# Modulation products, mLSTM weights and weight remainders placed elsewhere in a hybrid decoder layer

## The chip, the cores and the metric

One core of one Trainium2 chip runs the whole layer in one launch. The metric is device time in microseconds, the median of repeated runs. The engines are named as in the profile: PE (TensorE, matmuls), PEld (its weight loads), DVE (VectorE), ACT (ScalarE), POOL (GpSimd), SP (SyncE, which issues most of the transfers). Each engine, and each queue of transfers, takes its instructions in the order of the program; between engines semaphores carry the dependences.

## The reference

One decoder layer on x of 1024 positions by 1024 channels, everything in float32:

```
mod = silu(c) @ w_ada + b_ada                       # 6 rows of 1024: sh1 sc1 g1 sh2 sc2 g2
h   = rms_norm(x) * (1 + sc1) + sh1
proj = h @ w_in                                     # q,k of the mLSTM | v | o | gates | attention q | k,v
q_ml, k_ml = silu(causal conv of width 4 over positions)
h_ml = mLSTM(q_ml, k_ml, v_ml, gates)               # 4 heads of 128, max-stabilised
o_at = sliding window attention (8 heads of 64, window 128, rotary, sinks)
x   = x + g1 * rms_norm(concat(norms) @ w_out)
h   = rms_norm(x) * (1 + sc2) + sh2
x   = x + g2 * rms_norm((gelu(conv3(h @ w_up gate)) * conv3(h @ w_up value)) @ w_down)
```

The mLSTM's output for position t of a chunk is num / max(|den|, exp(-m_t)). In it the weight of an earlier position s is exp(b_t - b_s + i_s - m_t), and that of the state carried from earlier chunks is exp(b_t + m - m_t), where b is the running sum of the forget gate's logarithm and m_t the running maximum.

## The kernel before

Matrix products are made of float32 operands split into a part that TensorE takes in one pass (hi, a cast on ScalarE) and a remainder (lo = value - hi, a subtraction). `mm3` (L87) adds three products for each pair: hi by hi, hi by lo, lo by hi. So each weight tile of the input projection (a "unit", 128 x 1024, loaded whole by SP in `w_unit`, L139) needs a cast on ScalarE and a remainder, which units 0 to 9 form on VectorE and units 10 to 21 on GpSimd (L193). Raw, hi and lo tiles have three buffers each, so a unit takes the slot of the unit three before it.

The modulation vector is 48 columns of 128 values. `ada_sum` (L163) forms one of them on VectorE: it multiplies a 128 x 1024 tile of the transposed `w_ada` by silu(c), broadcast to all partitions in `cb`, and accumulates along the row.

The stages, in order:

1. Front (L197 to L411), in an order written out by hand on all engines (`manual_schedule`). Blocks of 128 positions of x are squared on ScalarE, scaled on VectorE (L261), transposed on TensorE (L265) and copied out of PSUM by both (L268). Two modulation sums, columns 8 and 0, end in `shift_gain` (L270); then the first 128 channels are modulated (L282), split and multiplied (L88 to L90). After that the channels go in eight chunks (`h_chunk`), with two sums, two splits and 48 matmuls each, for the attention's k and v and half of the mLSTM's v.
2. First token group (units 4 and 5: other half of v, gates). Keys are rotated (`rope`, VectorE and GpSimd), transposed and split in `kv_evac` (L449), all blocks ahead of the group's code.
3. Attention in two groups of four heads (units 6, 7 and 8, 9). After each block's front (`att_front`) one, in the second group two, modulation sums run in the background (`ada_bg`, L365: a load on SP into one of two buffers, and a sum). In the second group the gates are formed: `gates_rows` (L609) on 32 rows (head by block) and `gates_columns` (L653), which turns them into columns `gcol`. The row u = -max(...) goes to DRAM and returns broadcast to all partitions.
4. Four mLSTM heads (L771 to L783): two units with 512-column matmuls each, a convolution of four taps on ScalarE and VectorE (L690 to L695), and `ml_head` (L698). For each group of four blocks it forms the weights dm and qw (GpSimd addition, mask, ScalarE exponential, GpSimd multiplication), sq and kw on VectorE, and then block by block the numerator with its denominator column (`tot`), the state's increment (`st`), the state C on VectorE (L741, L743), and copies of `tot`: the numerator on ScalarE (L745), the denominator on VectorE (L746), the numerator's square on ScalarE (L748). Eight modulation sums stand between (L775, L781).
5. Output gates and output projection; then the feed-forward part, with seven products in place of eight.

Outside the stretches written by hand, a planner lays out each engine's order in advance, by simulated times and the order of the code; on the chip every engine keeps that order. `order(later, earlier)` adds a condition to it.

## Time and profile before

| | |
|---|---|
| median of 3 runs | 1149.92 us (1146.79 to 1153.52) |
| profiled execution | 1150.41 us, span 1148.7 us |
| mean granted TensorE clock | 0.991 |
| busy: PE, DVE, ACT, POOL | 97%, 75%, 49%, 18% of the span |

Windows and starts are microseconds from the start of the span. A group's row shows the line, engine and operation, the tiles (output <- inputs) with their shapes, the count, then busy time and mean nanoseconds of one, and last the idle time of the engine ahead of it with what ended it. A wait's row reads "who waited <- for whom: total, times, longest". A line of the timeline has start, duration, instruction, and in brackets the idle time before it.

### The profile page before, as it was taken

To read this page: it belongs to the slowest core of one execution; us is meant where nothing else is said; L and a number is where in the kernel's file an instruction comes from. 1 tells how busy PE (TensorE), PEld (TensorE's weight loads), DVE (VectorE), ACT (ScalarE), POOL (GpSimd) and SP (SyncE) were. 2 spreads that over 40 slices of the span, in tenths; PEclk is the share of its full clock that TensorE was granted. 3 is DMA by queue.
4 is the path that set the end of the run, shared out by engine and by line. 5 is a ranking of instruction groups with operands and counts; after the bars stand their busy time and mean duration, and the time that the engine had idled before them with its cause. 6 is when DMAs were issued, how large, how long until landed. Compare 5 with 4: busy or idle time off the path is not lost.

```text
span 1148.7 us, 16112 instructions
## 1 busy us (share of the span) xinstructions
PE 1114.7 (97%) x5919; PEld 941.1 (82%) x5919; DVE 857.9 (75%) x1501; ACT 564.1 (49%) x1112; POOL 203.8 (18%) x259
## 2 busy tenths in 40 slices
PE   6999999999999999999999999999999999999997
PEld 5999998777789888877788888888888888787885
DVE  6945889678764456799998797879787875787666
ACT  5642634524544446475554444545454554445552
POOL 3021447576665200000000000000000000000021
PEclk8999999999999999999999999999999999999999
DMA  9622445062111412333342233133313458553545
GB/s 359 237 83 75 130 123 186 25 202 70 42 37 35 150 74 92 110 95 107 120 121 81 92 127 111 57 118 119 120 56 110 141 194 289 169 173 119 173 119 200
DMA packets 54462, 144.72 MB, mean 126 GB/s; under 512 B 5304, under 2 KB 5616, under 8 KB 54384
## 3 DMA queue, kind: packets, MB, share of 16 engines
q1 hardware_dynamic: 52496, 138.19, 36.1%
q10 hardware_dynamic: 1888, 5.51, 1.2%
q8 instruction: 46, 0.75, 0.3%
q14 instruction: 32, 0.26, 0.1%
HBM read 115.09 MB, written 28.60 MB: 125 GB/s over the span
## 4 chain that ended last, share of the span: by engine, by line
PE 78%; DVE 12%; DMA 4%; ACT 2%; issue 2%; POOL 1%; SPq 1%; DVEq 0%; POOLq 0%; ACTq 0%
PE X L1005 7%; PE X L1004 7%; PE X L1003 7%; PE Y L1005 4%; PE Y L1003 4%; PE Y L1004 4%; DVE ada L164 3%; PE tg L88 3%; PE y L88 3%; PE y L90 3%; PE y L89 3%; PE tg L89 3%; PE tg L90 3%; DMA rb<-in_w_down_dram 2%; PE Z L1005 1%
## 5 line engine op out<-in xcount | busy, mean ns | idle before, releaser
L93 POOL TENSOR_SCALAR rsb<-ssb 128x1 f32<-128x1 f32 x4 | 2.3, 583 | 611.4 <-ACT junk L1228 611.2
L164 DVE SCALAR_TENSOR_TENSOR ada<-ada,cb 128x1024 f32<-128x1024 f32 x48 | 64.5, 1351 | 7.4 <-DMA ada<-in_w_ada_dram 7.2
L1003 PE MATMUL X<-S,wl 128*128 128x512 f32 x156 | 62.4, 400 | 0.0
L1005 PE MATMUL X<-S,wl 128*128 128x512 f32 x156 | 61.9, 396 | 0.0
L1004 PE MATMUL X<-S,wl 128*128 128x512 f32 x156 | 61.7, 395 | 0.0
L1013 DVE SCALAR_TENSOR_TENSOR yg<-ug,cv,yg 128x1023 f32<-128x1023 f32 (+1 forms) x44 | 56.4, 1281 | 5.7 <-ACT yg L1010 5.7
L85 ACT CAST wl<-T 128x512 fp32r<-128x512 f32 x41 | 25.5, 621 | 66.5 <-PE X L1004 62.6
L1013 DVE SCALAR_TENSOR_TENSOR yv<-uv,cv,yv 128x1023 f32<-128x1023 f32 (+1 forms) x44 | 56.3, 1278 | 1.9 <-ACT yv L1010 1.9
L85 ACT CAST w<-T 128x512 fp32r<-128x512 f32 x47 | 29.1, 623 | 40.7 <-PE Z L1005 34.7
L85 DVE TENSOR_TENSOR w<-T,w 128x512 fp32r<-128x512 f32 x47 | 32.1, 687 | 16.6 <-ACT w L85 16.6
L1057 DVE TENSOR_TENSOR uv<-q,X 128x512 f32<-128x512 f32 x22 | 15.1, 686 | 38.4 <-PE X L1005 38.4
L85 DVE TENSOR_TENSOR A<-ra,A 128x512 fp32r<-128x512 f32 x46 | 31.7, 689 | 15.9 <-ACT A L85 15.4
L85 ACT CAST A<-ra 128x512 fp32r<-128x512 f32 x46 | 28.6, 621 | 28.8 <-PE dxu L1177 14.2
L85 ACT CAST B<-rb 128x512 fp32r<-128x512 f32 x44 | 27.2, 619 | 31.0 <-DMA rb<-in_w_down_dram 13.9
L85 DVE TENSOR_TENSOR B<-rb,B 128x512 fp32r<-128x512 f32 x44 | 30.3, 689 | 10.0 <-ACT B L85 9.5
L1005 PE MATMUL Y<-S,wl 128*128 128x512 f32 x92 | 36.4, 396 | 0.0
L85 ACT CAST wl<-fu 128x512 fp32r<-128x512 f32 x21 | 13.0, 621 | 47.6 <-PE Y L1004 44.6
L1003 PE MATMUL Y<-S,wl 128*128 128x512 f32 x92 | 36.4, 395 | 0.0
L1004 PE MATMUL Y<-S,wl 128*128 128x512 f32 x92 | 36.2, 394 | 0.0
L1004 PEld LDWEIGHTS X<-S,wl 128*128 128x128 f32 x156 | 29.3, 188 | 7.6 <-issue 0.5
L1003 PEld LDWEIGHTS X<-S,wl 128*128 128x128 f32 x156 | 29.3, 188 | 7.5 <-issue 0.5
L1005 PEld LDWEIGHTS X<-S,wl 128*128 128x128 f32 x156 | 29.3, 188 | 7.1
(614 smaller groups left out, 4012.9 us busy)
## 6 DMA issues: line engine op xcount, KB each, us to landing
ada<-in_w_ada_dram SPq DMA_DIRECT2D x48, 512.0 KB, 4.4
ra<-a_dram SPq DMA_DIRECT2D x30, 512.0 KB, 3.7
fu<-in_w_up_dram SPq DMA_DIRECT2D x26, 512.0 KB, 3.6
a_dram<-yg SPq DMA_DIRECT2D x22, 512.0 KB, 3.7
rb<-in_w_down_dram SPq DMA_DIRECT2D x44, 256.0 KB, 3.6
fu_False<-in_w_up_dram SPq DMA_DIRECT2D x18, 512.0 KB, 3.6
a_dram<-s SPq DMA_DIRECT2D x11, 512.0 KB, 5.4
x<-in_x_dram SPq DMA_DIRECT2D x8, 512.0 KB, 7.3
```

The source lines that it names most:

```text
L85: return A.copy(hi, src), eng.tensor_tensor(lo, src, f(hi), op=ALU.subtract)
L88: T.matmul(ps, lh, rh, start=first, stop=False)
L89: T.matmul(ps, lh, rl, start=False, stop=False)
L90: return T.matmul(ps, ll, rh, start=False, stop=last)
L93: G.tensor_scalar(dst, ssq, 1.0 / n, EPS, op0=ALU.mult, op1=ALU.add)
L164: return V.scalar_tensor_tensor(w, w, 0.5, cb, op0=ALU.mult, op1=ALU.mult, accum_out=mod[:, j : j + 1])
L1003: T.matmul(ps, w[:, 0, ks], a[:, 0, k, :], start=st, stop=False, skip_group_check=True)
L1004: T.matmul(ps, w[:, 0, ks], a[:, 1, k, :], start=False, stop=False, skip_group_check=True)
L1005: ends = T.matmul(ps, w[:, 1, ks], a[:, 0, k, :], start=False, stop=en, skip_group_check=True)
L1013: V.scalar_tensor_tensor(t[:, sh:], src[:, : S - sh], w(tap), t[:, sh:], op0=ALU.mult, op1=ALU.add)
L1057: V.tensor_tensor(uv[:, 512:], p5, px_, op=ALU.add)
```

## The change

It has five parts.

- The front: columns 8 and 0 of the modulation are matrix products on TensorE (`ada_product`: for each of them eight matmuls of 128 x 128 by one column), with c loaded a second time as columns and the tiles of `w_ada` for these two laid out otherwise on the host. Three of the copies of the transposed x move from VectorE to ScalarE, the last of them behind the split of the first chunk.
- Key rotation (`k_turn`) and key split (`k_split`) stand inside the first token group's evacuation, block by block, with VectorE's order written out there; eight modulation sums stand there too, in place of those between the heads, and the splits of units 6 and 7 at its blocks 3 and 6.
- The remainders of units 10 to 21 are formed on VectorE.
- The mLSTM's second weight, exp(u + m), is formed once on 32 rows, and both rows are written to DRAM and broadcast, into two buffers; the mask is applied in place to the broadcast u, one instruction per head; the first weight is the exponential with the column a as bias, four instructions of 128 columns per group.
- The denominator is copied with the numerator by ScalarE, and VectorE takes its absolute value per block.

Two conditions of order are new: the gates' logarithm behind a mark of the first attention group's sixth block, and unit 8's remainder behind that of its third.

```diff
@@ -143,7 +146,7 @@
             s = slice(i * n, (i + 1) * n)
-            split(hi[:, s], lo[:, s], raw[:, s], eng)
+            rests[name] = split(hi[:, s], lo[:, s], raw[:, s], eng)[1]
         return hi, lo
@@ -190,7 +194,7 @@
             else:
-                units.append(w_unit(w_in[u if u < 4 else u - 2], 1024, f"w{u}", (G if u >= 10 else V,)))
+                units.append(w_unit(w_in[u if u < 4 else u - 2], 1024, f"w{u}"))
@@ -233,6 +237,7 @@
     nc.scalar.dma_start(ch8, c.rearrange("o (k m) -> (o k) m", k=KD))
+    nc.scalar.dma_start(cc8, ccol)
     x_load(0)
@@ -289,6 +294,9 @@
     V.scalar_tensor_tensor(ch8, th8, 1.0, ch8, op0=ALU.add, op1=ALU.mult)
+    A.activation(tc8, cc8, AF.Tanh, scale=0.5)
+    V.scalar_tensor_tensor(cc8, tc8, 1.0, cc8, op0=ALU.add, op1=ALU.mult)
+    V.tensor_scalar(cc8, cc8, 0.5, None, op0=ALU.mult)
     cbs = []
@@ -302,19 +310,29 @@
     x_evac(0, 1, D_)
+    mps = []
+    def ada_product(j):
+        if not mps:
+            mps.append(pA("mod0"))
+        for k in range(KD):
+            T.matmul(mps[0][:, j : j + 1], adas[j][:, k * P : (k + 1) * P], cc8[:, k : k + 1], start=k == 0, stop=k == KD - 1)
     for b in range(2, NB):
...
         x_evac(b - 2, 0, C_)
-        x_evac(b - 1, 1, D_)
+        x_evac(b - 1, 1, D_ if b < 6 else C_)
         if b == 5:
...
             V.scalar_tensor_tensor(gb, cv[:, C_BADA + 8 : C_BADA + 16], 1.0, cv[:, C_PREMIX : C_PREMIX + 8], op0=ALU.add, op1=ALU.mult)
-            ada_sum(8, adas[8])
+            ada_product(8)
         if b == 6:
-            ada_sum(0, adas[0])
-            shift_gain(0)
+            ada_product(0)
+    V.tensor_tensor(mod[:, 0:1], mps[0][:, 0:1], cv[:, C_BADA : C_BADA + 1], op=ALU.add)
+    V.scalar_tensor_tensor(g_mix[:, 0:1], mps[0][:, 8:9], cv[:, C_PREMIX : C_PREMIX + 1], gb[:, 0:1], op0=ALU.mult, op1=ALU.add)
     h0, h1 = h_part(0, 0), h_part(0, 1)
@@ -328,8 +346,8 @@
     h1[2]()
-    x_evac(7, 1, D_)
     h1[3]()
+    x_evac(7, 1, C_)
@@ -446,13 +464,18 @@
-    def kv_evac(b, ps):
-        kr = ap_.tile([P, 256], F32, tag="qr", bufs=2, name=f"kr{b}")
+    krs = {}
+    def k_turn(b):
+        ps = pkv[b // 2][:, 256 * (b % 2) : 256 * (b % 2 + 1)]
+        kr = krs[b] = ap_.tile([P, 256], F32, tag="qr", bufs=2, name=f"kr{b}")
         rope(kr[:, :P].rearrange("p (h t f) -> p h t f", h=2, t=2),
...
         A.copy(vat[:, b, :, :64], ps[:, P : 2 * P].rearrange("p (v d) -> p v d", v=2))
+    def k_split(b):
         pk = pB(f"pk{b}")
-        T.transpose(pk[:, :P], kr[:, :P], ident)
+        T.transpose(pk[:, :P], krs[b][:, :P], ident)
         ts = slice(b * P, (b + 1) * P)
@@ -543,21 +566,31 @@
+    second = tc.manual_schedule(engines={mybir.EngineType.DVE})
+    second.__enter__()
     ensure(6)
...
         v_evac(b, 1, pv[b // 2][:, 256 * (b % 2) : 256 * (b % 2 + 1)])
-    for b in range(NB):
-        kv_evac(b, pkv[b // 2][:, 256 * (b % 2) : 256 * (b % 2 + 1)])
     def v_gates(b, ps):
...
         A.copy(gates.rearrange("p (g b) -> p g b", g=8)[:, :, b], ps[:, 256:264])
+        if b + 2 < NB:
+            k_turn(b + 2)
+        k_split(b)
+        if b == 6:
+            ensure(8)
+        ada_bg(ap_)
+        if b == 3:
+            ensure(7)
...
         G.memset(mix_v(b)[:, :, HD : HD + 1], vscale)
+    k_turn(0)
+    k_turn(1)
     token_group(4, VG, v_gates)
     V.tensor_tensor(gates.rearrange("p (g b) -> p g b", g=8), gates.rearrange("p (g b) -> p g b", g=8), bc(rw[:, 0:8], 2, [P, 8, NB]), op=ALU.add)
-    ensure(7)
+    ensure(8)
+    second.__exit__(None, None, None)
@@ -579,9 +612,8 @@
-    ensure(8)
     att_group(6, 0)
-    gcol = cp.tile([P, 5, 32], F32, name="gcol")
+    gcol = cp.tile([P, 4, 32], F32, name="gcol")
@@ -592,7 +624,7 @@
-    V.scalar_tensor_tensor(tA, gf_, -1.0, gf_, op0=ALU.mult, op1=ALU.min)
+    order(V.scalar_tensor_tensor(tA, gf_, -1.0, gf_, op0=ALU.mult, op1=ALU.min), marks[5])
     A.activation(tA, tA, AF.Exp)
@@ -641,7 +674,10 @@
         V.tensor_scalar(urow, crow, mprev, -1.0, op0=ALU.max, op1=ALU.mult)
-        nc.sync.dma_start(u_dram, urow)
+        A.activation(erow, urow, AF.Exp, bias=mprev)
+        for i, r in enumerate((urow, erow)):
+            nc.sync.dma_start(u_dram[i], r)
         V.tensor_tensor(brow, urow, brow, op=ALU.subtract)
@@ -657,14 +693,13 @@
         V.tensor_scalar(t2, ident[:R, :R], t1[:, 0:1], None, op0=ALU.mult)
-        V.tensor_scalar(t3, ident[:R, :R], mprev, None, op0=ALU.mult)
         T.matmul(pg2[:, 96:128], ones[:R, :], t2, start=True, stop=True)
-        T.matmul(pg2[:, 128:160], ones[:R, :], t3, start=True, stop=True)
-        V.tensor_copy(gcol, pg2[:, 0:160].rearrange("p (a b) -> p a b", a=5))
-    a_c, fl_c, ws_c, dec_c, mp_c = (gcol[:, i, :] for i in range(5))
+        V.tensor_copy(gcol, pg2[:, 0:128].rearrange("p (a b) -> p a b", a=4))
+    a_c, fl_c, ws_c, dec_c = (gcol[:, i, :] for i in range(4))
     ensure(10)
+    order(rests["w8"], marks[2])
     att_group(8, 1)
@@ -696,26 +731,24 @@
     def ml_head(h, q, k):
-        ub = lp.tile([P, NB, P], F32, tag="U", bufs=1, name=f"U{h}")
+        ub = lp.tile([P, 2, NB, P], F32, tag="U", bufs=2, name=f"U{h}")
         nc.sync.dma_start(
-            ub.rearrange("p a b -> p (a b)"),
-            u_dram[8 * h : 8 * h + 8, :].rearrange("(o a) b -> o (a b)", o=1).to_broadcast([P, S]),
+            ub.rearrange("p i a b -> p i (a b)"),
+            u_dram[:, 8 * h : 8 * h + 8, :].rearrange("i a b -> i (a b)").unsqueeze(0).to_broadcast([P, 2, S]),
         )
+        G.affine_select(ub[:, 0], ub[:, 0], pattern=[[0, NB], [1, P]], compare_op=ALU.is_ge, fill=NEG, base=0, channel_multiplier=-1)
         sums = lp.tile([P, 8], F32, tag="sums", bufs=2, name=f"sums{h}")
-        den = lp.tile([P, 8], F32, tag="mden", bufs=2, name=f"mden{h}")
         tmp = lp.tile([P, 8], F32, tag="mtmp", bufs=2, name=f"mtmp{h}")
...
             cs = slice(8 * h + 4 * g, 8 * h + 4 * g + 4)
-            us = ub[:, 4 * g : 4 * g + 4, :]
+            us, es = (ub[:, i, 4 * g : 4 * g + 4, :] for i in range(2))
             dm = lp.tile([P, 4, P], F32, tag="dm", bufs=2, name=f"dm{h}_{g}")
-            G.tensor_tensor(dm, us, bc(a_c[:, cs], 2, [P, 4, P]), op=ALU.add)
-            G.affine_select(dm, dm, pattern=[[0, 4], [1, P]], compare_op=ALU.is_ge, fill=NEG, base=0, channel_multiplier=-1)
-            A.activation(dm, dm, AF.Exp)
+            for i in range(4):
+                c = 8 * h + 4 * g + i
+                A.activation(dm[:, i, :], us[:, i, :], AF.Exp, bias=a_c[:, c : c + 1])
             qw = lp.tile([P, 4, P], F32, tag="qw", bufs=2, name=f"qw{h}_{g}")
-            G.tensor_tensor(qw, us, bc(mp_c[:, cs], 2, [P, 4, P]), op=ALU.add)
-            A.activation(qw, qw, AF.Exp)
-            G.tensor_tensor(qw, qw, q[:, 512 * g : 512 * (g + 1)].rearrange("p (a b) -> p a b", a=4), op=ALU.mult)
+            G.tensor_tensor(qw, es, q[:, 512 * g : 512 * (g + 1)].rearrange("p (a b) -> p a b", a=4), op=ALU.mult)
             pS = pA(f"mS{h}_{g}")
@@ -742,14 +775,14 @@
                     Cst = Cn[:, : HD + 1]
-                A.copy(mix_chunk(b, h), tot[:, :HD])
-                V.tensor_copy(den[:, b : b + 1], tot[:, HD : HD + 1])
+                A.copy(mix_v(b)[:, h, : HD + 1], tot[:, : HD + 1])
+                de = mix_v(b)[:, h, HD : HD + 1]
+                V.scalar_tensor_tensor(tmp[:, b : b + 1], de, -1.0, de, op0=ALU.mult, op1=ALU.max)
                 jk = lp.tile([P, P], F32, tag="jk", bufs=1, name=f"jk{h}_{b}")
...
             gs = slice(4 * g, 4 * g + 4)
-            tm, de, sm = tmp[:, gs], den[:, gs], sums[:, gs]
-            V.scalar_tensor_tensor(tm, de, -1.0, de, op0=ALU.mult, op1=ALU.max)
+            tm, sm = tmp[:, gs], sums[:, gs]
             V.tensor_tensor(tm, tm, fl_c[:, cs], op=ALU.max)
@@ -772,14 +805,10 @@
         q = conv_chunk(u, h, f"q{h}")
-        for _ in range((2, 1, 1, 1)[h]):
-            ada_bg(lp)
         u += 1
...
         u += 1
-        for _ in range((0, 1, 1, 1)[h]):
-            ada_bg(lp)
         ml_head(h, q, k)
@@ -1302,11 +1331,17 @@
     )
+    w_ada = np.ascontiguousarray(g["w_ada"][0].T)
+    for j in (0, 8):
+        b = slice(j * P, (j + 1) * P)
+        w_ada[b] = g["w_ada"][0][:, b].reshape(KD, P, P).transpose(1, 0, 2).reshape(P, D)
     rows = np.concatenate([g["ml_i_b"][0], g["ml_f_b"][0], g["attn_sinks"][0]])[None, :]
...
         "x": g["x"].reshape(S, D),
-        "w_ada": g["w_ada"][0].T,
+        "w_ada": w_ada,
         "c": g["c"].reshape(1, D),
+        "ccol": _columns(g["c"]),
         "w_vg": w_vg,
```

More of the change, by code (lines that the diff above doesn't have):

```diff
@@ L63, in layer_kernel @@
     c: bass.AP,
+    ccol: bass.AP,
     w_vg: bass.AP,
@@ L109, in layer_kernel @@
     g_dram = drp.tile([2, D], F32, name="g_dram")
-    u_dram = drp.tile([32, P], F32, name="u_dram")
+    u_dram = drp.tile([2, 32, P], F32, name="u_dram")
     x1_dram = drp.tile([S, D], F32, name="x1_dram")
@@ L137, in w_pair @@
         return tuple(wp.tile([P, 4 * VG], F32R, tag=part, bufs=3, name=f"{name}{part}") for part in ("hi", "lo"))
+    rests = {}
     def w_unit(src, w, name, engs=(V,), dst=None):
@@ L155, in layer_kernel @@
     ch8, th8 = (ap0.tile([KD, P], F32, name=n) for n in ("ch8", "th8"))
+    cc8, tc8 = (ap0.tile([P, KD], F32, name=n) for n in ("cc8", "tc8"))
     V.memset(ones, 1.0)
@@ L617, in gates_rows @@
         urow = cut(608, P)
+        erow = cut(896, P)
         V.tensor_copy(irow, pg[:R, 0:P])
```

## The prediction

> **What bounds the kernel now.** The engine totals were read first, then the stretches, then TensorE's waits in the stretches with gaps, then the order of time around each wait. Totals of busy time by engine:
>
> ```profile
> PE 1114.7 (97%) x5919; PEld 941.1 (82%) x5919; DVE 857.9 (75%) x1501; ACT 564.1 (49%) x1112; POOL 203.8 (18%) x259
> ```
>
> Span 1148.7 us, so TensorE is idle for only 34 us. The stretches say where. Columns: length, then busy time of the five engines, granted TensorE clock, DMA share, GB/s:
>
> ```profile
> 20.00:40.00 20.00, 17.53 (x117) 16.40 (x118) 19.26 (x38) 9.79 (x15) 1.02 (x3) 0.83 0.97 374
> 64.00:100.00 36.00, 36.00 (x303) 36.00 (x302) 10.76 (x38) 13.90 (x45) 6.74 (x19) 1.00 0.21 67
> 155.00:211.00 56.00, 52.55 (x401) 46.11 (x399) 49.42 (x132) 26.00 (x78) 31.66 (x37) 0.96 0.49 153
> 250.00:345.00 95.00, 86.47 (x496) 73.06 (x495) 75.75 (x133) 42.92 (x114) 65.15 (x62) 0.98 0.19 63
> 195.00:200.00 5.00, 5.00 (x28) 4.05 (x26) 4.79 (x11) 3.01 (x11) 3.58 (x5) 0.66 0.46 161
> 210.00:215.00 5.00, 5.00 (x18) 3.82 (x18) 3.36 (x6) 3.93 (x11) 2.28 (x3) 0.66 0.38 110
> 335.00:340.00 5.00, 4.36 (x24) 4.17 (x23) 3.74 (x13) 2.42 (x8) 1.35 (x3) 0.66 0.01 3
> ```
>
> Three things: the front (20 to 40) has VectorE full; 64 to 100, the first token group, has TensorE full and VectorE mostly free; attention's second half and the mLSTM heads have 3.45 and 8.53 us of TensorE gaps, with three places where the clock falls to 0.66. In each of these 5 us, 0.34 x 5 = 1.7 us of work is lost beside the gap, 5.1 in all. Who ends the gaps (TensorE's waits, 176 to 345 us; total, times, longest):
>
> ```profile
> PE st L738 <- DVE C L741: 2.5, 2, 1.4
> PE tot L735 <- DVE C L743: 2.3, 2, 1.7
> PE pt L515 <- ACT sm L507: 1.8, 1, 1.8
> PE po L528 <- POOL pN L522: 1.7, 1, 1.7
> PE st L738 <- DVE kw L728: 1.2, 1, 1.2
> PE cvq L88 <- ACT ubk L687: 0.7, 1, 0.7
> PE tot L733 <- ACT jk L748: 0.4, 1, 0.4
> ```
>
> No line here waits for a matmul's data from memory; all wait for a small VectorE, ScalarE or GpSimd step. Why these steps are late is seen in order of time (start, duration, idle before):
>
> ```profile
> 189.85 2.39 POOL L85 TENSOR_TENSOR w12lo<-w12raw,w12hi 128x1024 fp32r<-128x1024 f32 x1
> 194.68 0.44 PE L528 MATMUL po<-vat,pN 128*128 128x65 f32 x2 [1.70 <-POOL pN L522]
> 206.90 2.37 POOL L85 TENSOR_TENSOR w13lo<-w13raw,w13hi 128x1024 fp32r<-128x1024 f32 x1
> 207.05 2.24 DVE L505 SCALAR_TENSOR_TENSOR ngm<-mx,nsink 128x4 f32<-128x4 f32 x1
> 209.78 0.33 PE L515 MATMUL pt<-ident,sm 128*128 128x128 f32 x1 [1.75 <-ACT sm L507]
> ...
> 332.76 1.46 POOL L718 TENSOR_TENSOR qw<-qw,yq 128x512 f32<-128x512 f32 x1 [0.74 <-ACT qw L717]
> 333.02 1.22 DVE L752 SCALAR_TENSOR_TENSOR mtmp<-mden 128x4 f32<-128x4 f32 x1
> ```
>
> A weight remainder on GpSimd takes 2.4 us. w12's stands in GpSimd's queue ahead of attention's mask, and TensorE waits 1.70 us. w13's holds up a VectorE instruction on four columns until it ends (2.24 us), the exponentials follow late, and TensorE waits 1.75 us. So an elementwise step on GpSimd stalls VectorE while it runs. The groups of the heads (211 to 345 us; the 128-column exponential and one unhindered split from wider windows):
>
> ```profile
> L692 DVE SCALAR_TENSOR_TENSOR yq<-ubq,cv,yq 128x1024 f32<-128x1024 f32 x12 | 21.1, 1756 | 2.7 <-ACT yq L690 2.6
> L164 DVE SCALAR_TENSOR_TENSOR ada<-ada,cb 128x1024 f32<-128x1024 f32 x8 | 13.2, 1656 | 5.9 <-DMA ada<-in_w_ada_dram 5.9
> L752 DVE SCALAR_TENSOR_TENSOR mtmp<-mden 128x4 f32<-128x4 f32 x6 | 3.9, 643 | 0.1
> L746 DVE COPY mden<-tot 128x1 f32<-128x1 f32 x24 | 3.5, 150 | 4.4 <-ACT mix L745 4.4
> L507 ACT ACTIVATE sm<-sm,ngm 128x128 f32<-128x128 f32 x64 | 20.5, 391 | 26.9 <-DVE ngm L505 26.8
> L85 DVE TENSOR_TENSOR w9lo<-w9raw,w9hi 128x1024 fp32r<-128x1024 f32 x1 | 1.2, 1218 | 0.0
> L712 POOL TENSOR_TENSOR dm<-U,gcol 128x512 f32<-128x512 f32 x8 | 13.2, 1661 | 6.7 <-PE mK L724 4.9 <-DMA U<-u_dram 1.6 <-DVE sq L726 0.2
> L716 POOL TENSOR_TENSOR qw<-U,gcol 128x512 f32<-128x512 f32 x8 | 10.9, 1366 | 2.9 <-PE tot L735 2.8
> ```
>
> The convolution taps take 1.76 us where the same 1024 columns need 1.22 elsewhere, and VectorE's queue stands 5.9 us waiting for modulation weights, with the state updates behind it.
>
> **The change, part by part.** Sums go against the profiled execution's own 1150.41 us (span 1148.7 and 1.7 around it), which lies 0.5 above the median of 1149.92.
>
> *The two GpSimd sums and the twelve remainders.* Forming the weights on 32 rows takes the two 512-column additions per group off GpSimd: 13.2 + 10.9 = 24.1 us. The remainders w10 to w21 take off twelve times 2.4, 28.8 us. The mask stays, the same elements in one instruction per head. With the eight modulation sums (13.2 us, and 5.9 us of waits) out of VectorE's queue too, the makers of five wait rows go: 2.5 + 2.3 + 1.8 + 1.7 + 1.2 = 9.5 us, and with the gaps the three clock drops, 5.1. Together -14.6; bounds 0 (a later step takes each place) and -14.6.
>
> *Denominators.* ScalarE now copies 129 columns and VectorE reads them from SBUF, so the square of the numerator no longer queues behind a VectorE copy of the same bank:
>
> ```profile
> ACT jk L748 <- DVE mden L746: 20.0, 13, 4.2
> ```
>
> ScalarE loses 20 us of waiting, which ends the two ScalarE rows above: -1.1; bounds 0 and -1.1.
>
> *What comes onto VectorE.* Twelve remainders at 1.22 us, 14.6 us, in place of sums at 1.66. In the queue they stand ahead of state updates as the sums did. Among 32 such long instructions (24 taps, 8 sums) five waits on VectorE arose in the heads, which would make two of twelve; I take three, since a split also waits for its cast: +3.7. Bounds 0 and +14.6. The 32 small instructions for the denominators stand in for 32 copies of 0.15, and eight instructions go: nothing; if they stretch to L752's 0.64, the idle 19 us of VectorE (75.75 of 95 busy) hide it, and without that cover it is 32 x 0.49 = 16 us.
>
> By the Trainium skill, page "SBUF — State Buffer", section "Who interferes with whom", a VectorE instruction with two SBUF inputs is blocked by a GpSimd one that reads SBUF, while one with at most one SBUF input is not. The trace agrees: 150 ns for the copy from PSUM, 643 for the two-input row. That speaks against this part, as the new denominators and remainders all have two SBUF inputs and the multiplication that held L752 for 1.22 us stays; at the old rate a fifth of those 16 us on the path would make the sum 3 worse. GpSimd's load falls by more than half (65.15, less 24.1 and some seven remainders of 2.4), so I leave it out.
>
> *Exponentials.* 32 of 128 columns at 0.39 (12.5 us) for 16 of 512 columns, which cost no less each (6.2 or more): at most +6.3 us on a ScalarE that is busy 42.92 of 95, so nothing. The 32-row exponential and a second 16 KB write stand on the gates' path well before the first head; the broadcast doubles to 1 MB but has two buffers: nothing; if the first head waits for it, twice the 1.6 us in L712's row.
>
> *Modulation sums into the first token group.* Eight at 1.22, plus w7, on a VectorE that has 25 us free there: nothing; their loads pass the w6 and w7 loads on SP's queue, and VectorE now keeps program order, so behind a late sum stand the key splits and w7's remainder, which the first query group needs. Without the cover, the 5.9 us that sums waited in the heads. The gate logarithms and w8's remainder move behind blocks of the first query group, both needed only by the second: nothing, or one split of 1.22.
>
> *The front.* VectorE loses two sums and three copies; TensorE gains 16 matmuls of two passes each:
>
> ```profile
> 17.99 1.06 PE L265 MATMUL xtp<-ident,x 128*128 128x128 f32 x8 [0.20 <-DVE x L261]
> 18.51 1.22 DVE L164 SCALAR_TENSOR_TENSOR ada<-ada,cb 128x1024 f32<-128x1024 f32 x1
> 23.28 1.94 PE L265 MATMUL xtp<-ident,x 128*128 128x128 f32 x8 [1.66 <-DVE x L261]
> 23.65 0.54 DVE L282 TENSOR_SCALAR xT<-xT,gains,mod 128x512 f32<-128x512 f32 x1
> 32.86 0.69 DVE L284 TENSOR_TENSOR hTlo<-xT,hThi 128x512 fp32r<-128x512 f32 x1 [0.39 <-ACT hThi L283]
> ...
> 143.24 1.51 PE po L528 x14
> ...
> 6.04 3.78 PE L297 MATMUL cb<-ch,ident 8*128 8x128 f32 x16 [6.04 <-DVE ch L291]
> ```
>
> A pass with one moving column has no row. Nearest is the 65-column one, 1.51/14 = 0.108 us, so 16 passes 1.73. TensorE's new order is block 5, product, block 6, product, block 7: 17.99 + 1.06 + 1.73 + 1.06 + 1.73 = 23.6, then two one-column steps like L746's, 0.15 each, and a handover like the 0.20 ahead of 17.99: the first modulated tile starts at 24.1 instead of 23.65: +0.5. What follows it up to the second chunk's remainder at 32.86 stays a VectorE chain, so TensorE's first products, warmer or not, wait there. Bounds: with no time for the products, 23.65 less two sums is 21.2: -2.4. At the cold row, 3.78 each with block 6 at 1.94, 29.1: +5.5. I take +0.5, since the products fill the gap (1.66) after which eight transposes took 1.94 instead of 1.06. The second load of c, its tanh and two column steps come ahead of block 0, while loads set the pace; uncovered, 0.15 x 3.
>
> Sum: -14.6 - 1.1 + 3.7 + 0.5 = -11.5, 1138.9; on the median's scale 1138.4, said as 1139.
>
> By the Trainium skill, page "TensorE: Matmul & The Clock Gate", section "Part 1: The HAM clock gate (the "warmup" mystery)", the clock falls after an idle window of about 3.4 us. The trace disagrees: 0.66 follows gaps of 1.70 and 1.75 us. By the page the 5.1 us would not be had and the sum would be -6.4; the measurement decides.
>
> **Rivals.**
> *All gaps go.* With both queues freed, the splits find room in VectorE's new slack, also ahead of the output weights: -14.6 - 1.1 - 2.4 (front) = -18.1, 1132. For: a remainder is needed only by the next unit but one, the state updates at once. Against: the front's products.
> *Half goes.* TensorE's order was laid out in advance, and new late producers stand where old ones stood: half of 14.6, front +0.5, splits +3.7: -3.1, 1147. For: the taps, 1.2 us each, still stand ahead of the state updates.
> *Slower: the remainders clog VectorE.* A remainder needs ScalarE's cast, which needs the slot of the unit three back; such a wait held GpSimd before, now it holds VectorE and the state updates behind it:
>
> ```profile
> ACT w15hi L85 <- PE cvq L89: 6.9, 1, 6.9
> ACT w14hi L85 <- PE cvk L89: 2.2, 1, 2.2
> ```
>
> Price: 14.6 of splits and 9.1 of waits, all on the path, less 14.6 and 1.1, front +0.5: +8.5, 1159. It makes the kernel slower only once over 21 of the 23.7 us reach TensorE. Against: head waits of VectorE on such casts have not reached TensorE so far.
> *The front is cold:* likeliest sum with +5.5, 1144.
>
> **How the numbers follow.** Likeliest 0.50 (alone 1133 to 1145), all gaps 0.20, half 0.18, clogged 0.08, cold front 0.04. A half per cent, 5.7 us, is about what can be told from no change; so faster means under 1144.2: 0.47 + 0.20 + 0.03 = 0.70; same 0.21; slower 0.09. The range of 1128 to 1152 takes in the second case with 4 us below it and the half case with 5 above; the clogged case is left out.
>
> **What would show it.** Right: no clock of 0.66 between 180 and 345 us; TensorE's gaps in the heads under 4 us; taps near 1.3 us; no ScalarE wait on denominators; the first tile at 24 us, give or take 1; 64 to 100 still full. Wrong: VectorE idle for casts of w12 to w19 with state updates behind; a gap at the first query group for w7; a cold front with the first tile after 27.

## The result, and the profile after

The changed kernel takes 1132.95 us (median; 1130.74 to 1133.66) where the kernel before takes 1148.91 beside it. The ratio is 0.9852 with a 95% interval of 0.9833 to 0.9871: 16.0 us less. The profiled execution of the changed kernel took 1133.66 us with a span of 1131.9, so the two profiles differ by 16.8 us of span. The forecast was 1139, 11.5 us less.

The engine totals of the changed kernel:

```profile
PE 1112.1 (98%) x5949; PEld 943.5 (83%) x5949; DVE 838.3 (74%) x1499; ACT 564.0 (50%) x1133; POOL 148.4 (13%) x227
```

TensorE is idle for 1131.9 - 1112.1 = 19.8 us instead of 34.0, and GpSimd works 55 us less. The same stretches of the changed kernel as those shown for the kernel before (length, busy time of the five engines, granted clock, DMA share, GB/s):

```profile
20.00:40.00 20.00, 19.27 (x138) 18.81 (x139) 15.80 (x34) 11.40 (x19) 0.21 (x2) 0.83 0.94 366
64.00:100.00 36.00, 36.00 (x302) 36.00 (x301) 17.67 (x51) 13.21 (x44) 6.91 (x17) 1.00 0.48 155
155.00:211.00 56.00, 55.87 (x418) 49.59 (x418) 50.65 (x136) 27.04 (x77) 27.71 (x36) 1.00 0.52 161
195.00:200.00 5.00, 5.00 (x37) 4.11 (x37) 5.00 (x19) 3.22 (x12) 2.32 (x4) 1.00 0.59 211
210.00:215.00 5.00, 5.00 (x35) 4.00 (x34) 5.00 (x13) 3.33 (x9) 2.58 (x3) 1.00 0.01 2
250.00:345.00 95.00, 95.00 (x629) 86.28 (x628) 61.64 (x138) 43.85 (x137) 37.20 (x50) 1.00 0.13 40
335.00:340.00 5.00, 5.00 (x45) 5.00 (x45) 2.81 (x11) 1.44 (x7) 2.32 (x6) 1.00 0.00 0
```

The 3.45 us of TensorE gaps in attention's second half are down to 0.13, the 8.53 in the heads to nothing, and neither stretch has a fall of the clock any more. The front still has its low clock, and 64 to 100 us is full in spite of the eight sums that VectorE now does there. TensorE's waits over the whole run now have no row of attention or of the heads' state updates left:

```profile
PE cb L305 <- DVE ch L296: 5.9, 1, 5.9
PE dz L1204 <- ACT wl L86: 2.1, 1, 2.1
PE dx L1205 <- DVE B L86: 1.0, 3, 0.6
PE tg L89 <- DVE mix L800: 0.8, 2, 0.4
PE xtp L270 <- DVE x L266: 0.8, 3, 0.3
PE kv L89 <- ACT hThi L288: 0.7, 1, 0.7
PE dx L1205 <- DVE wl L86: 0.2, 1, 0.2
```

Where the time came off is read from when one kind of product starts for the last time. The last product with the heads' state and the first of the feed-forward's large products, before and then after (duration least, median and most in ns, then first and last start in us):

```profile
L735 PE MATMUL tot<-C,qw x56: 271/275/484, 256.0 to 363.0; 128*128 128x129 f32 x56
L1003 PE MATMUL X<-S,wl x156: 389/394/802, 538.3 to 926.4; 128*128 128x512 f32 x156
```

```profile
L768 PE MATMUL tot<-C,qw x56: 271/275/276, 247.0 to 345.0; 128*128 128x129 f32 x56
L1032 PE MATMUL X<-S,wl x156: 392/396/793, 519.9 to 907.4; 128*128 128x512 f32 x156
```

The heads end 18.0 us sooner, and at 907.4 against 926.4 the lead is 19.0. About 2 us of it are given back after that, at the second down projection. There TensorE waits for a weight load and its cast, and then loses clock (first the stretches, TensorE alone, then the matmul that ends the wait):

```profile
966.00:969.00 3.00, 0.87 (x4) 1.00 0.23 85
969.00:973.00 4.00, 4.00 (x12) 0.57 0.62 188
```

```profile
968.35 0.47 PE L1204 MATMUL dz<-B,A 128*128 128x512 f32 x1 [2.13 <-ACT wl L86]
```

### The profile page after: what moved, and what is told of

Its sections match the earlier page's. It is cut to its first block, busy times and chain, and to the rows that moved or that the text cites. A ratio compares the mean times of both kernels' runs of the same rounds, so it can differ in the third digit from the quotient of the medians.

```text
span 1131.9 us, 16163 instructions
## 1 busy us (share of the span) xinstructions
PE 1112.1 (98%) x5949; PEld 943.5 (83%) x5949; DVE 838.3 (74%) x1499; ACT 564.0 (50%) x1133; POOL 148.4 (13%) x227
## 4 chain that ended last, share of the span: by engine, by line
PE 90%; DVE 4%; DMA 3%; issue 1%; ACT 1%; POOL 0%; SPq 0%; DVEq 0%; POOLq 0%; ACTq 0%
PE X L1033 7%; PE X L1032 7%; PE X L1034 7%; PE Y L1033 4%; PE Y L1034 4%; PE Y L1032 4%; PE tg L89 3%; PE tg L90 3%; PE tg L91 3%; PE y L89 3%; PE y L90 3%; PE y L91 3%; PE po L551 2%; DMA rb<-in_w_down_dram 2%; PE Z L1034 1%; PE Z L1032 1%
## 5 line engine op out<-in xcount | busy, mean ns | idle before, releaser
L168 DVE SCALAR_TENSOR_TENSOR ada<-ada,cb 128x1024 f32<-128x1024 f32 x46 | 56.8, 1244 | 2.5 <-DMA ada<-in_w_ada_dram 2.4
L86 DVE TENSOR_TENSOR A<-ra,A 128x512 fp32r<-128x512 f32 x46 | 31.7, 689 | 16.8 <-ACT A L86 16.7
```

Of the source, the lines that this page charges most:

```text
L86: return A.copy(hi, src), eng.tensor_tensor(lo, src, f(hi), op=ALU.subtract)
L168: return V.scalar_tensor_tensor(w, w, 0.5, cb, op0=ALU.mult, op1=ALU.mult, accum_out=mod[:, j : j + 1])
```

## The experiments

The theory from the prediction is that GpSimd's elementwise work and the modulation sums in VectorE's queue made the small steps late for which TensorE waits. Its rivals: one part alone does it all, or some part gives its gain back elsewhere. The ratio is to the kernel before on the same chip; its median was 1148.9 to 1151.7 us there, so differences between rows of some 2 us are read from the ratios. "Idle" is the length of the stretch less TensorE's busy time in the profiled execution.

| kernel | time, us | ratio to before | idle 155 to 211 | idle 250 to 345 |
|---|---|---|---|---|
| before | 1150.2 (29 runs) | 1 | 3.45 | 8.53 |
| changed | 1132.95 | 0.9852 [0.9833, 0.9871] | 0.13 | 0.00 |
| changed, remainders back | 1142.52 | 0.9932 [0.9911, 0.9953] | 2.94 | 1.94 |
| changed, weights back | 1134.48 | 0.9871 [0.9856, 0.9886] | 0.23 | 0.42 |
| changed, denominators back | 1133.78 | 0.9862 [0.9839, 0.9884] | 0.00 | 0.16 |
| changed, products back | 1133.46 | 0.9862 [0.9843, 0.9880] | 0.00 | 0.00 |
| changed, sums back | 1135.91 | 0.9879 [0.9862, 0.9897] | 0.45 | 1.24 |
| remainders alone | 1146.16 | 0.9960 [0.9945, 0.9976] | 2.05 | 6.57 |
| sums' move alone | 1140.27 | 0.9919 [0.9900, 0.9939] | 3.09 | 1.09 |
| weights, denominators alone | 1143.15 | 0.9923 [0.9899, 0.9947] | 3.61 | 4.97 |
| remainders and sums' move | 1136.90 | 0.9886 [0.9867, 0.9906] | 0.44 | 1.18 |
| changed, products 128 wide | 1133.16 | 0.9844 [0.9823, 0.9865] | 0.08 | 0.00 |

### The remainders back on GpSimd

```diff
-                units.append(w_unit(w_in[u if u < 4 else u - 2], 1024, f"w{u}"))
+                units.append(w_unit(w_in[u if u < 4 else u - 2], 1024, f"w{u}", (G if u >= 10 else V,)))
```

> The changed kernel with the remainders of units 10 to 21 back on GpSimd, all else kept. Theory (remainders on GpSimd block VectorE and attention's masks): the two gaps and two clock drops of attention's second half come back, 1.70 + 1.75 + 3.4 us, and some 2 us in the heads, so about 1141 us, with TensorE waiting for the mask and for the exponentials between 180 and 215 us. Rival (the gain came from the sums that left the heads or from the denominators): at most 2 us back, 1133 to 1135, heads and attention without gaps.

Measured: 1142.52 us, 9.6 more than the changed kernel. Its stretches, and its order of time where attention's gaps are back (start, duration, idle before):

```profile
155.00:211.00 56.00, 53.06 (x409) 47.09 (x409) 47.78 (x135) 25.34 (x78) 33.37 (x39) 1.00 0.48 152
250.00:345.00 95.00, 93.06 (x578) 82.16 (x577) 65.00 (x127) 45.94 (x143) 52.15 (x53) 1.00 0.18 56
```

```profile
197.97 0.62 PE L538 MATMUL pt<-ident,sm 128*128 128x128 f32 x2 [1.06 <-ACT sm L530]
...
201.63 0.44 PE L551 MATMUL po<-vat,pN 128*128 128x65 f32 x2 [1.83 <-POOL pN L545]
```

Both waits of the kernel before, for the mask and for the exponentials, return with this one edit, so they are the remainders' doing. The theory's 1141 us is nearly met, but not by its terms: its two clock drops (3.4 us) did not come back, as the 1.00 in both stretches shows. Of the 9.6 us the profiled execution shows 4.75 as additional idle time in the two stretches, and 2.3 as a later first key-value product (26.80 instead of 24.48), which goes with a longer stretch of half clock in the front and not with this edit (below). The rest stays open: between the last of attention's products and the last of the heads TensorE is busy some 2.8 us longer.

### The weights back on 128 rows

```diff
-            for i in range(4):
-                c = 8 * h + 4 * g + i
-                A.activation(dm[:, i, :], us[:, i, :], AF.Exp, bias=a_c[:, c : c + 1])
+            G.tensor_tensor(dm, us, bc(a_c[:, cs], 2, [P, 4, P]), op=ALU.add)
+            G.affine_select(dm, dm, pattern=[[0, 4], [1, P]], compare_op=ALU.is_ge, fill=NEG, base=0, channel_multiplier=-1)
+            A.activation(dm, dm, AF.Exp)
...
-            G.tensor_tensor(qw, es, q[:, 512 * g : 512 * (g + 1)].rearrange("p (a b) -> p a b", a=4), op=ALU.mult)
+            G.tensor_tensor(qw, us, bc(mp_c[:, cs], 2, [P, 4, P]), op=ALU.add)
+            A.activation(qw, qw, AF.Exp)
+            G.tensor_tensor(qw, qw, q[:, 512 * g : 512 * (g + 1)].rearrange("p (a b) -> p a b", a=4), op=ALU.mult)
...
```

> The changed kernel with the old way of forming the mLSTM weights (two additions and a mask per group on GpSimd, one broadcast row, one buffer), all else kept. Theory (GpSimd additions hold VectorE in the heads): gaps of 1.0 to 2.7 us before state updates and one clock drop come back, 3 to 6 us, 1136 to 1139. Rival (with the remainders gone GpSimd has room enough): within 1 us of the changed kernel, 1132 to 1134, convolution taps still under 1.45 us.

Measured: 1134.48 us, 1.5 more, with intervals that overlap, and nearer to the rival than to the theory: with the other parts in place, the 24 us of additions that left GpSimd are worth little. What they do to VectorE is seen in the denominators' step (one column, both inputs in SBUF), in the heads of the changed kernel, of this one, and of the one with the remainders back:

```profile
L780 DVE SCALAR_TENSOR_TENSOR mtmp<-mix 128x1 f32<-128x1 f32 x31 | 6.4, 208 | 11.9 <-ACT mix L778 11.8
```

```profile
L780 DVE SCALAR_TENSOR_TENSOR mtmp<-mix 128x1 f32<-128x1 f32 x29 | 9.1, 327 | 5.5 <-ACT mix L778 5.3
```

```profile
L780 DVE SCALAR_TENSOR_TENSOR mtmp<-mix 128x1 f32<-128x1 f32 x27 | 11.6, 435 | 4.2 <-ACT mix L778 4.1
```

The same instruction takes 208 ns where GpSimd is busy for 37.20 of the 95 us, and 327 and 435 where it is busy for 51.21 and 52.15. The load alone does not order the last two; the slower one is that with the remainders of 2.4 us among GpSimd's steps. The Trainium skill, page "SBUF — State Buffer", section "Who interferes with whom", says that a VectorE instruction with two SBUF inputs contends with a GpSimd one that reads SBUF, and these rows agree.

### The denominators back in VectorE's copy

```diff
-                A.copy(mix_v(b)[:, h, : HD + 1], tot[:, : HD + 1])
-                de = mix_v(b)[:, h, HD : HD + 1]
-                V.scalar_tensor_tensor(tmp[:, b : b + 1], de, -1.0, de, op0=ALU.mult, op1=ALU.max)
+                A.copy(mix_chunk(b, h), tot[:, :HD])
+                V.tensor_copy(den[:, b : b + 1], tot[:, HD : HD + 1])
...
```

> The changed kernel with the denominator copied from PSUM by VectorE, all else kept. Theory: ScalarE waits on VectorE again (some 10 to 20 us in the heads) but only about 1 us reaches TensorE, 1134. Rival (the waits of ScalarE were what held PSUM and the state chain): 4 us or more, 1137 and up.

Measured: 1133.78 us, 0.8 more, which this measurement cannot tell from nothing. ScalarE waits for VectorE's copies again, 17 times and 9.6 us in all, and in the profiled execution TensorE is idle 0.16 us in the heads. So in this kernel what ScalarE waits there stays hidden, as the theory has it.

### The first pair as sums again

```diff
-            ada_product(8)
+            ada_sum(8, adas[8])
...
-            ada_product(0)
+            ada_sum(0, adas[0])
+            shift_gain(0)
...
-    for j in (0, 8):
+    for j in ():
```

> The changed kernel with the first two modulation columns summed on VectorE as before and three copies back on VectorE, all else kept. By the forecast (products cost 0.5 us) 1132.4; by the trace of the changed kernel (first modulated tile at 23.18 instead of 23.65) 1133.4; either way within 1 us of it. Rival (the front carries a visible part of the gain): 1135 or more. First modulated tile back at about 23.6 us.

Measured: 1133.46 us, 0.5 more: no difference that can be told. Its profile has an unlooked-for row. At 165 us, in attention, the clock falls to half with no gap before it (the stretches, then one of the last instructions ahead of the fall):

```profile
162.00:165.00 3.00, 3.00 (x27) 2.59 (x26) 2.10 (x7) 0.91 (x3) 1.39 (x4) 1.00 0.67 194
165.00:168.00 3.00, 3.00 (x18) 2.77 (x19) 2.65 (x5) 0.38 (x1) 0.20 (x1) 0.51 0.64 199
```

```profile
164.11 0.39 PE L546 MATMUL po<-vat,pT 128*128 128x65 f32 x2
```

From 161.7 to 165.4 nearly all of TensorE's work is score products on 64 of 128 rows and products 65 columns wide. It shows as busy throughout, and still the clock falls. In the profiled execution with the denominators back the clock falls at the end of the same series, at 167.4 us, also without a gap. The other ten profiles have no such fall there, though the changed kernel's has the same series, so the series alone does not decide it.

### The remainders alone

```diff
-                units.append(w_unit(w_in[u if u < 4 else u - 2], 1024, f"w{u}", (G if u >= 10 else V,)))
+                units.append(w_unit(w_in[u if u < 4 else u - 2], 1024, f"w{u}"))
```

This one is made from the kernel before.

> The kernel before with one edit: the remainders of w10 to w21 go to VectorE, everything else stays. Taking this edit back from the changed kernel cost 9.6 us (1142.52 against 1132.95). Theory A, the GpSimd remainders by themselves make most of the gaps (they stand ahead of the masks and hold VectorE while they run): the same 8 to 11 us come off the kernel before, 1139 to 1142, the gaps at pN L522 and ngm L505 go and with them the clock drops at 195 and 210. Rival B, the remainders only find room on VectorE because the modulation sums have left its queue: here both stand in it, the heads keep their waits for the state updates (C L741, L743) or have more of them, and the time is 1146 to 1151.

Measured: 1146.16 us, 3.8 less than before, inside rival B's window (its lower edge) and far from theory A's. The stretch of the heads, and two of TensorE's waits in it:

```profile
250.00:345.00 95.00, 88.43 (x523) 75.00 (x522) 76.09 (x145) 45.26 (x119) 58.72 (x61) 1.00 0.21 67
```

```profile
PE tot L733 <- ACT jk L748: 2.7, 4, 1.1
PE tot L735 <- DVE C L743: 1.2, 2, 0.9
```

In the heads 6.57 of the 8.53 us of idle time remain. The waits for C are 2.3 us in all where they were 4.8, and those for ScalarE's square of the numerator 2.7 where they were 0.4. In attention the makers have changed. The sums now stand ahead of the scores' evacuation on the same VectorE, and the mask waits behind another GpSimd step:

```profile
185.19 1.20 DVE L164 SCALAR_TENSOR_TENSOR ada<-ada,cb 128x1024 f32<-128x1024 f32 x1
...
186.33 0.77 DVE L503 COPY_PREDICATED sm<-later,s 128x256 f32<-128x256 uint32 x2
...
186.90 0.35 PE L494 MATMUL s<-khi,qhi 64*128 64x256 f32 x1 [0.48 <-DVE sm L503]
186.91 1.93 POOL L541 TENSOR_SCALAR mix<-mix,rsta 128x512 f32<-128x512 f32 x1
...
189.49 0.44 PE L528 MATMUL po<-vat,pN 128*128 128x65 f32 x2 [1.30 <-POOL pN L522]
```

So the remainders' edit does not stand by itself. Rival B has the time, and its reason in part: the heads keep most of their idle time, but only half of their waits for the state updates.

### The sums' move alone

The changed kernel with the edits of the four experiments above that put a part back (remainders, weights, denominators, products), so that the sums' move, the key splits and VectorE's written order are what is left:

```diff
+            if b + 2 < NB:
+                k_turn(b + 2)
+            k_split(b)
...
+            ada_bg(ap_)
```

> The changed kernel with remainders, weights, denominators and front products all as before; what is left of the change is that the eight modulation sums, with the key splits and the order of VectorE's queue, stand in the first token group. Theory A (remainders carry most): little comes of it, 1144 to 1148, with the two attention gaps at the mask and the exponentials and their clock drops still there, and the heads' waits for C smaller than the 4.8 us of before. Rival B (the sums' place carries as much): 1139 to 1142.

Measured: 1140.27 us, 9.7 less than before, as rival B has it. The idle time in the heads falls from 8.53 us to 1.09; in attention 3.09 of 3.45 remain, and the clock is at 0.94:

```profile
155.00:211.00 56.00, 52.91 (x381) 46.55 (x380) 46.60 (x131) 24.18 (x72) 33.65 (x38) 0.94 0.48 151
250.00:345.00 95.00, 93.91 (x580) 82.83 (x579) 65.98 (x133) 44.19 (x122) 67.55 (x70) 1.00 0.16 51
```

GpSimd is as loaded here as before (67.55 of 95 us), the `yq` taps still take 1.76 us each, and still the heads run almost full. So it was enough to change what stands in VectorE's queue; GpSimd's load alone does not make the heads wait. The sums' new place, the key splits' and VectorE's written order were not tried one by one.

### Weights and denominators alone

The changed kernel with remainders, sums and products put back, and one buffer instead of two for the broadcast rows; the sums' edit is, in part,

```diff
-        ada_bg(ap_)
...
         q = conv_chunk(u, h, f"q{h}")
+        for _ in range((2, 1, 1, 1)[h]):
+            ada_bg(lp)
...
```

> The changed kernel with remainders, modulation sums and front products as before: of the change only the weights formed on 32 rows and the denominators are left. Remainders alone gave 3.8 us, the sums' move alone 9.7, both 13.1. Theory: weights and denominators relieve the same state updates in the heads as the sums' move does, so alone they give clearly more than the 4 us they add on top of the other two: 1140 to 1144, with attention's two gaps still there (pN L545, sm L530) and the waits on C in the heads under 2 us. Rival: they need the other two, since remainders on GpSimd and sums in VectorE's queue still hold the state updates: 1145 to 1148.

Measured: 1143.15 us, a ratio of 0.9923 (8.5 us under 1151.66, the median of before beside it): inside the theory's window. The heads' idle time only falls from 8.53 us to 4.97, though, and one wait on C is longer than the theory's 2 us:

```profile
250.00:345.00 95.00, 90.03 (x552) 78.48 (x551) 73.68 (x139) 44.04 (x135) 49.45 (x52) 1.00 0.28 95
```

```profile
PE mK L751 <- DVE C L770: 2.6, 1, 2.6
```

Alone the two are worth 0.81% (the sums' move) and 0.77%, but not by the same gaps: the sums' move nearly empties the heads of idle time, the weights and denominators take away less than half of it. Part of their gain is the clock, whose mean is 0.995 in this profiled execution for 0.991 before; how the rest comes about is not shown. With the sums moved and the remainders on GpSimd (the first experiment against "sums' move alone"), weights, denominators and products add nothing that shows: 0.9932 against 0.9919.

### Remainders and the sums' move together, and everything but the sums' move

The first is the changed kernel with weights, denominators and products put back.

> The changed kernel with weights, denominators and front products as before: only the remainders on VectorE and the sums' move are left. Singly, these three cost 1.5, 0.8 and 0.5 us when taken back. If they add up, 1135 to 1137. Rival: with both the GpSimd additions and the denominators' copies back together, VectorE's small steps are held often enough that the state updates come late again: 1138 to 1143, with waits of TensorE on C or kw in the heads.

Measured: 1136.90 us, where the sum of the two parts alone (3.8 + 9.7) gives 1136.5 and adding up the three small parts gave 1135 to 1137. The second is the changed kernel with the sums' edit of the last experiment, and one buffer instead of two for the broadcast rows.

> The changed kernel with the eight modulation sums back between the heads (and one buffer instead of two for the broadcast rows, which the room needs). Theory: the sums and their wait for loads stood ahead of state updates, so the waits on C (2.5 + 2.3 us before) come back in part: 1136 to 1140. Rival: with GpSimd nearly empty VectorE has enough slack that a sum delays nobody: within 1.5 us of the changed kernel, 1132 to 1134.5, with TensorE's gaps in the heads under 1.5 us.

Measured: 1135.91 us, 3.0 more than the changed kernel, between the two: just under the theory's 1136 and above the rival's 1134.5, with the idle time in the heads under the rival's 1.5 us. The heads of the one and of the other:

```profile
250.00:345.00 95.00, 93.82 (x609) 84.13 (x608) 66.49 (x147) 46.97 (x131) 54.17 (x66) 1.00 0.13 40
```

```profile
250.00:345.00 95.00, 93.76 (x611) 83.92 (x609) 69.81 (x155) 45.95 (x146) 38.31 (x51) 1.00 0.23 75
```

In both, attention is nearly full (0.44 and 0.45 us idle), and 1.2 us is left in the heads. By the table, attention is full to within 0.5 us in every kernel with the remainders on VectorE but the one made from the kernel before (2.05), and in none with them on GpSimd (2.9 to 3.6). The heads come down to 1.1 to 1.9 us with the sums moved and one or both of the other parts (the remainders; weights and denominators) left out, and to 1.24 by those two parts together without the sums' move. So the heads' gap can be closed from two sides; only with all of them is nothing left.

### The front's products 128 columns wide

```diff
-            T.matmul(mps[0][:, j : j + 1], adas[j][:, k * P : (k + 1) * P], cc8[:, k : k + 1], start=k == 0, stop=k == KD - 1)
+            T.matmul(mps[0][:, 16 * j : 16 * j + P], adas[j][:, k * P : (k + 1) * P], cc8[:, k : k + 1].to_broadcast([P, P]), start=k == 0, stop=k == KD - 1)
...
```

> The changed kernel with the front's 16 passes 128 columns wide instead of one (the column of c is broadcast, the first column of the result is used). In the profiles so far the clock stood at half speed for 7.0, 10.4, 7.0, 10.4 and 3.6 us of the front where the one-column passes were there, and for 7.0, 3.6, 3.6, 3.6 and 0 us where they were not. Theory: a stretch of one-column passes counts as idle for the clock although TensorE shows as busy; with 128 columns the passes take some 0.13 us each instead of 0.115, the half-speed stage of the front is 3.6 us or less, the first key-value product starts at 24.3 to 25.2 us, and the median falls by 0 to 1.5 us, to 1131.5 to 1133. Rival: the width does not matter (the transposes around them are what counts as idle): half speed for 7 to 10 us again, the first product at 24.5 to 26.9, 1133 to 1134.

Measured: 1133.16 us, ratio 0.9844: no difference from the changed kernel, and in the rival's window. The front in order of time, of the changed kernel, of the one with the remainders back, and of this one:

```profile
18.36 1.84 PE L320 MATMUL mod<-cc,ada 128*128 128x1 f32 x16
20.07 1.07 PE L270 MATMUL xtp<-ident,x 128*128 128x128 f32 x8
20.97 1.84 PE L320 MATMUL mod<-cc,ada 128*128 128x1 f32 x16
22.68 1.07 PE L270 MATMUL xtp<-ident,x 128*128 128x128 f32 x8
24.48 0.58 PE L89 MATMUL kv<-w0hi,hThi 128*128 128x256 f32 x1 [0.73 <-ACT hThi L288]
```

```profile
21.73 3.41 PE L320 MATMUL mod<-cc,ada 128*128 128x1 f32 x16
25.00 1.95 PE L270 MATMUL xtp<-ident,x 128*128 128x128 f32 x8
26.80 0.58 PE L89 MATMUL kv<-w0hi,hThi 128*128 128x256 f32 x1
```

```profile
20.93 1.95 PE L320 MATMUL mod<-cc,ada 128*128 128x128 f32 x16
...
24.55 0.39 PE L89 MATMUL kv<-w0hi,hThi 128*128 128x256 f32 x1 [0.79 <-ACT hThi L288]
...
32.48 0.39 PE L89 MATMUL kv<-w0hi,hThi 128*128 128x256 f32 x1 [1.24 <-ACT hThi L288]
```

The wide passes cost 1.95 us for 1.84, and in this execution the front had no half-speed stage at all; with one-column passes the stages were 6.8, 10.2, 6.8, 10.2 and 3.4 us long. The front is as the theory has it, but in one profile, and the profiled executions with sums in the front had stages of 6.8, 3.4, 3.4, 3.4 and 6.8 us and once none, so the width is not shown to be the cause. The gain does not arrive for another reason: TensorE gets through its first products faster and then waits 1.24 us at 32.48 for the second chunk, whose cast and VectorE steps come ahead of it, as the prediction said of any warmer front.

## Why the prediction was right, and where it was wrong

**The GpSimd sums, the remainders and the modulation sums (-14.6).** The mechanism held and was priced a little low. Idle time in the two stretches fell by 3.45 + 8.53 - 0.13 = 11.85 us, where the named waits were 9.5 (and 1.1 for the denominators), and the three clock drops there, 5.1 us, are gone. Over the two whole profiles TensorE's idle time fell by 14.2 us (34.0 to 19.8). What the step left unsaid is that the parts do not share the sum by their instructions' time. Remainders alone give 3.8 us, the sums' move alone 9.7, weights with denominators alone 8.5, all together 16.0. Where a gap has two makers the parts overlap: the 24.1 us that the additions took on GpSimd brought 1.5 once the others were in. The remainders go the other way: 3.8 us alone, 3.4 on top of the sums' move, 9.6 as the last part, of which some 2.3 are the front's clock and 2.8 are unexplained.

**The three clock drops as a fixed 5.1 us.** In attention and the heads of the two profiles this was right, as a rule it was not. The execution with the remainders back had a gap of 1.83 us at 201.63 and kept full clock; a gap of 1.70 us in the same stretch cost the kernel before a drop; and the drop at 165 us came without a gap. Such a stretch is followed by a drop only in some executions. In the profiled execution of the changed kernel another drop came later, at the second down projection. By the two profiles' mean clocks, 0.991 of 1148.7 us and 0.993 of 1131.9, the lost clock is an estimated 10.3 and 7.9 us: of the 16.8 us there some 2.4 are clock and 14.2 are gaps. Over all runs the mean granted clock was 0.991 before (0.987 to 0.996, 29 runs) and 0.996 after (0.993 to 0.999, four runs), by which an estimated 10.3 and 4.5 us are lost, so that up to 6 of the 16 us are clock and some 10 are gaps.

**The denominators (-1.1).** Taking them back cost 0.8 us, less than the intervals are wide (0.9839 to 0.9884 against 0.9833 to 0.9871). The ScalarE wait is gone as forecast; whether it was worth 1.1 is not shown.

**The remainders on VectorE (+3.7).** This is the step that failed: no such loss is seen. The wait that it feared is there and reaches no one:

```profile
L86 DVE TENSOR_TENSOR w14lo<-w14raw,w14hi 128x1024 fp32r<-128x1024 f32 x1 | 1.6, 1559 | 3.5 <-ACT w14hi L86 3.5
L86 DVE TENSOR_TENSOR w15lo<-w15raw,w15hi 128x1024 fp32r<-128x1024 f32 x1 | 1.2, 1226 | 2.7 <-ACT w15hi L86 2.7
L727 DVE SCALAR_TENSOR_TENSOR yq<-ubq,cv,yq 128x1024 f32<-128x1024 f32 x10 | 12.8, 1282 | 0.5 <-ACT yq L725 0.4
```

VectorE stands 3.5 and 2.7 us at casts, and TensorE is busy for all 95 us of the heads. Carrying the old kernel's rate of waits over was the error: those waits came with the sums in VectorE's queue and their loads (with the sums' move alone the heads' idle time is down to 1.09 us) and with a VectorE held by GpSimd (`yq` taps of 1.76 us, now 1.28). With both gone it has 95 - 61.64 = 33 us free, and the updates follow in time. For the same reason the 3 us by the Trainium skill's rule on two-input instructions (page "SBUF — State Buffer", section "Who interferes with whom") were rightly left out of the sum, though the rule itself is seen at work in the 208, 327 and 435 ns.

**Exponentials and sums at nothing.** Right: ScalarE is busy 43.85 us in the heads for 42.92 before, and the first token group is full with VectorE at 17.67 of 36 us.

**The front (+0.5).** The price of the products was right (1.84 us for an estimated 1.73), and the sign was wrong in the profiled execution: the first product started at 24.48 for 24.95 before, since block 5's transposes began at 17.46 and not 17.99. In the other four profiles of kernels with one-column products it started between 24.85 and 26.88, so no fixed price can be given; taking them back changed the time by 0.5 us, within the measurement. That the products, by filling the gap, would keep the transposes behind them at full clock held here (1.07 us) and in one more profile; in three they took 1.95. Here too the clock fell right after: 5.4 us of one-column passes and transposes, all shown as busy, and 0.73 us of waiting were followed by 6.8 us at half clock, and in those three the clock fell while passes and transposes ran. The cold front forecast as a rival was there in these, with up to 3.41 us for a product. It cost 1.6 to 2.4 us at the first product, not the 5.0 that lay between the two sums, and it was not made up later: with the remainders back the last products for k and v start at 75.3 us for 72.9.

**Not foreseen:** the 2 us given back at the second down projection. There the wait for a weight's load and cast was 1.6 us before and 2.1 after, and after it a half-speed stage followed. In all twelve profiles that wait lies between 0.6 and 2.1 us, and the stage follows the four longest (1.9 to 2.1: the changed kernel, remainders back, products back, products 128 wide) and none of the eight others (0.6 to 1.8). So here the drop goes with the length of the wait; why the wait is longer in these four is not shown.

**The rivals.** What came is nearest to the first: all gaps go, 1132, at the chance of 0.20; 1132.95 lies just below the likeliest case's own 1133 to 1145. Its mechanism held for the gaps and the splits. That its size fits so well is partly luck: its 2.4 us at the front came to 0.5, the gaps gave more than its 15.7, and some 2 us were lost again later. Half the gaps staying was wrong. Clogging was wrong, though its sign (VectorE idle at casts) is in the profile.

**The clock gate.** The Trainium skill, page "TensorE: Matmul & The Clock Gate", section "Part 1: The HAM clock gate (the "warmup" mystery)", was set aside in the prediction because gaps of 1.70 and 1.75 us were followed by a drop. That was half a reading. The page also says that the window of about 3.4 us is free-running, and the traces agree with this: every half-speed stage ahead of the end lasts 3.41, 6.83 or 10.24 us, one, two or three windows. They disagree with an idle window as the condition, since drops followed gaps of half that length, and in two profiles a stretch of narrow products without any gap.

## What to carry to other kernels

Where an engine's gaps have several makers, the gains of the parts do not add up: price a part by what remains when the others are in. It can then bring less than alone (weights and denominators) or more (the remainders, 9.6 us for 3.8). A rate of waits counted in the old kernel must not be carried over to new instructions once the change takes away what made those waits; ask how much free time the engine has left in that stretch, here 33 of 95 us. Treat a clock drop after a gap of this length as a chance and not as a fixed price: a gap of 1.7 us was followed by 1.7 us of lost clock in one profile and a gap of 1.8 us by none in another.

## What the runs showed of the hardware that was not expected

The clock can fall though TensorE shows as busy. After 3.3 us of products on 64 rows or 65 columns wide it fell to half for 3.4 us, in two of twelve profiles, and in three it fell among one-column passes and transposes of the front. Half-speed stages ahead of the end come in whole multiples of 3.41 us, and the same series of products is followed by one in some profiles and not in others. That is probably part of the 2 to 7 us by which times of one kernel differ: the run of the changed kernel with a mean clock of 0.999 took 1130.74 us, the one with 0.993 took 1133.66.

A matmul pass with one moving column was hardly cheaper than one with 128: 1.84 us against 1.95 for 16.
